# Eight heads' output matmuls in one bank: all products of the rows first, then all products of the state, one clearing matmul for each half of the partitions

## The chip, the cores and the metric

The kernel runs on one core of a Trainium2 chip. The metric is the device time of one execution in microseconds (us); the figure that counts is the median of the timed runs. All profile rows come from one profiled execution of the kernel before.

## The reference, cut to what matters

The model is two blocks of 256 tokens with 1024 channels. The second block has a recurrent layer (the function `wkv7_scan`) with 16 heads of 64 channels. Per head there is a 64 x 64 state, and for each token

```
sa = einsum('bhij,bhj->bhi', S, a_t)
S = S * w_t + sa[..., None] * b_t + v_t[..., None] * k_t
y_t = einsum('bhij,bhj->bhi', S, r_t)
```

The kernel computes this in chunks of 64 tokens. For a chunk and a head the output y is a sum of two products: one of the chunk's own rows (values v and corrections u, against a masked 128 x 64 matrix), and one of the state that the chunk before left behind (64 x 64, against the chunk's queries). The first chunk has no state, so it has the first product alone.

## The kernel before, in words

The program is traced as one long list of instructions for each engine, and a planner puts each engine's list in an order at build time: an instruction that was traced earlier goes first when it is ready by the planner's reckoning, and a later one may fill a gap. On the chip each engine takes its list in that order.

Work runs through these stages: the first block, a feed-forward layer, the recurrent layer (function `rwkv`), feed-forward, feed-forward, attention, feed-forward. The change touches the last part of `rwkv`. There the 16 heads are two halves A = 0 and A = 1 of eight heads. These generators are stepped in a written order, the string `OB`:

- `chain(A)` is the recurrence over the four chunks, in order: L1150 (state times a, on TensorE), L1152 (VectorE adds it into the tile `u`), L1157 (inverse times u), L1159 (ScalarE copies the result back into `UV`), L1165 (the new state's increment), L1173 (VectorE makes the new state).
- `outputs(A)` takes, for each chunk `ch`, a PSUM bank, runs the matmuls for eight heads (four pairs `i`, two heads `e` of a pair in the two halves of the partitions), and has ScalarE copy the bank into `Y` (L1188). L1185 is the product of the rows: 128 rows of contraction, 64 columns of output, written "128*64" in the rows. L1187 is the product of the state: 64 rows, 64 columns, "64*64"; e = 0 uses the upper left quarter of the array, e = 1 the lower right one.
- `finish(j)` turns `Y` into the layer's normalised and gated output (L1223 transposes, L1232 centring, L1236 and L1237 gate, L803 sums of squares, then VectorE and ScalarE).
- `out_part` multiplies by the output weights (L126, three products per weight block).

```
OB="cocooocccfccfccOffcOOOFFppppFFqqrr"
RB={..., "o": "AAB", "t": "AAB", "fv": "AAB", "fc": "C", "fg": "AAB", ...}
env = {"c": chain(1), "o": outputs(0), "f": chained(finish(0), finish(1)), "p": p0, "O": outputs(1),
       "F": chained(finish(2), finish(3)), "q": part(1), "r": part(2)}
```

So `o` are the four chunks of the first half's outputs, `O` those of the second half; three of the four `O` stand in a row, and behind them `F` and then `p`. `OB` is the tracing order; the planner keeps near to it. The banks of `o` and `O` go round A, A, B (two buffers of A, one of B). All these operands are 32-bit floats; a matmul of such operands shows as two records of MATMUL in the trace (and two of LDWEIGHTS).

A matmul with `start=True` clears the bank's accumulation in the partitions it writes, one without adds to what was written since the last clearing, or overwrites where nothing was.

Of the kernel before, what the change touches and what calls it, by code (L numbers as in the profile page):

```python
# [49 lines left out]
class Builder:  # L50
# [759 lines left out]
    def rwkv(self, x, ss):  # L810
        nc, tc, a = self.nc, self.tc, self.a
        self.banks = {**BANKS, **RB}
        LC = float(np.exp(-0.5))
        with tc.tile_pool(name="rwkv", bufs=1) as pool:
# [114 lines left out]
            AR = [five(ARb[c // 4])[:, c % 4] for c in range(NC)]  # L929
# [119 lines left out]
            UVp, UV = [], []  # L1049
# [9 lines left out]
            PM = [None, None]  # L1059
# [117 lines left out]
            def outputs(A):  # L1177
                hp0 = 4 * A
                for ch in range(4):
                    par, cp, S = ch % 2, ch // 2, states[A][ch]  # L1180
                    by = self.bank("o")[:, :T].rearrange("p (i t) -> p i t", i=4)
                    for i in range(4):
                        for e in range(2):
                            er, h = slice(64 * e, 64 * e + 64), 2 * (hp0 + i) + e
                            nc.tensor.matmul(by[er, i], UV[ch][:, h], PM[A][1][:, ch, 2 * i + e], start=True, stop=S is None)  # L1185
                            if S is not None:
                                nc.tensor.matmul(by[er, i], S[er, i], AR[hp0 + i][er, ch, 1], start=False, stop=True)  # L1187
                    nc.scalar.activation(Y[:, hp0:hp0 + 4, 64 * ch:64 * ch + 64], by, AF.Copy)  # L1188
                    yield

# [13 lines left out]
            def finish(j):  # L1204
# [40 lines left out]
                for e in range(2):  # L1245
# [6 lines left out]
            part = lambda i: self.out_part(x, a["rk_o"], i, yh, yl)  # L1252
            p0 = part(0)
            env = {"c": chain(1), "o": outputs(0), "f": chained(finish(0), finish(1)), "p": p0, "O": outputs(1),
                   "F": chained(finish(2), finish(3)), "q": part(1), "r": part(2)}
            for o in OB:
# [293 lines left out]
```

## Time and profile before

| what | us |
|---|---|
| median of 3 runs | 2389.93 |
| the runs | 2403.57, 2389.93, 2389.66 |
| profiled execution | 2403.91 |
| its span, first to last instruction | 2401.9 |
| TensorE busy in the span | 2286.2 |
| VectorE busy | 1558.1 |
| ScalarE busy | 1086.7 |

The profiled execution is 14.0 us above the median. Times in the rows count from the start of its span. "PE" is TensorE, "DVE" VectorE, "ACT" ScalarE, "POOL" GpSimd. PEclk is the granted clock of TensorE as a share of 2.4 GHz (0.50 is 1.2 GHz).

### The profile page before, as it was taken

The page shows a single profiled execution, that of the slowest core. Times are in us where ns is not written, and L with a number is a line of the kernel's source. Part 1 is how long each engine was busy: PE and PEld are TensorE (multiplying, and loading weights), DVE is VectorE, ACT ScalarE, POOL GpSimd, SP SyncE. Part 2 cuts the span into 40 slices and gives each one's busy share as a digit, 9 for nine tenths or more (in the row PEclk, how much of TensorE's full clock was granted, in tenths as well). Part 3 has the DMA queues.
Part 4 walks back from the last instruction along what each step waited for, and adds up shares of the span by engine and source line. Part 5 has one row for each costly group of instructions (what it writes and reads, how often), then busy time and mean ns, then how long its engine had stood idle before and what let it go on. Part 6 is the DMA issues. An engine that isn't in the chain of part 4 may idle for free.

```text
span 2401.9 us, 48629 instructions
## 1 busy us (share of the span) xinstructions
PE 2286.2 (95%) x20688; PEld 2171.1 (90%) x20688; DVE 1558.1 (65%) x2387; ACT 1086.7 (45%) x1501; POOL 319.1 (13%) x226
## 2 busy tenths in 40 slices
PE   4999898999999989999999789999999999999999
PEld 3888898999999989999999678878999999888999
DVE  7667579448854497555765777325665765787664
ACT  4344444443344433445544554423544644555543
POOL 3001379500000000000000543211000000101000
PEclk7889899999999999999999788967999999999999
DMA  7766444554455535555556222202556556433555
GB/s 252 243 197 201 150 159 158 189 180 141 143 187 187 179 115 163 187 185 167 175 185 178 83 91 64 84 1 70 181 181 187 182 185 184 155 106 107 185 185 148
DMA packets 107756, 378.33 MB, mean 158 GB/s; under 512 B 12113, under 2 KB 15697, under 8 KB 107410
## 3 DMA queue, kind: packets, MB, share of 16 engines
q1 hardware_dynamic: 104224, 370.52, 48.2%
q10 hardware_dynamic: 3314, 4.70, 0.6%
q8 instruction: 162, 2.65, 0.5%
q14 instruction: 56, 0.46, 0.1%
HBM read 374.12 MB, written 1.05 MB: 156 GB/s over the span
## 4 chain that ended last, share of the span: by engine, by line
PE 77%; DVE 6%; POOL 2%; ACT 1%; issue 1%; POOLq 0%; DVEq 0%; ACTq 0%
PE bkA L126 25%; PE bkA L572 15%; PE bkB L126 11%; PE bkC L750 10%; PE bkD L750 4%; DVE wlo L100 1%; POOL wlo L100 1%; POOL b L865 1%; PE bkC L1349 1%; DVE e L718 1%; PE bkA L1185 1%; ACT whi L99 1%; PE bkB L731 0%; PE bkE L731 0%; DVE ep L722 0%
## 5 line engine op out<-in xcount | busy, mean ns | idle before, releaser
L99 ACT ACTIVATE whi<-raw 128x1024 fp32r<-128x1024 f32 (+1 forms) x664 | 695.6, 1048 | 999.7 <-PE bkA L126 284.8
L100 DVE TENSOR_TENSOR wlo<-raw,whi 128x1024 fp32r<-128x1024 f32 (+1 forms) x606 | 733.4, 1211 | 480.1 <-ACT whi L99 449.7
L126 PE MATMUL bkA<-xh,whi 128*128 128x256 f32 x1336 | 332.0, 287 | 14.8 <-ACT whi L112 7.0
L126 PE MATMUL bkA<-xl,whi 128*128 128x256 f32 x1336 | 331.4, 288 | 12.4 <-POOL xl L316 6.3
L126 PEld LDWEIGHTS bkA<-xh,whi 128*128 128x128 f32 x1336 | 255.7, 192 | 18.2 <-ACT whi L112 7.7
L126 PEld LDWEIGHTS bkA<-xl,whi 128*128 128x128 f32 x1336 | 255.5, 193 | 16.3 <-POOL xl L316 8.7
L572 PE MATMUL bkA<-xh,whi 128*128 128x256 f32 x1024 | 259.9, 290 | 0.0
L572 PE MATMUL bkA<-xl,whi 128*128 128x256 f32 x1024 | 251.6, 281 | 0.0
L572 PEld LDWEIGHTS bkA<-xl,whi 128*128 128x128 f32 x1024 | 193.3, 189 | 0.0
L572 PEld LDWEIGHTS bkA<-xh,whi 128*128 128x128 f32 x1024 | 193.2, 189 | 0.0
L126 PE MATMUL bkA<-xh,wlo 128*128 128x256 f32 x1336 | 187.4, 282 | 2.5 <-DVE wlo L100 2.5
L100 POOL TENSOR_TENSOR wlo<-raw,whi 128x1024 fp32r<-128x1024 f32 x58 | 155.6, 2694 | 197.0 <-DVE on L149 128.7
L126 PEld LDWEIGHTS bkA<-xh,wlo 128*128 128x128 f32 x1336 | 171.0, 190 | 3.1 <-DVE wlo L100 2.9
L126 PE MATMUL bkB<-xh,whi 128*128 128x256 f32 x624 | 157.3, 289 | 1.9 <-ACT whi L99 1.1
L572 PE MATMUL bkA<-xh,wlo 128*128 128x256 f32 x1024 | 149.7, 284 | 7.5 <-POOL wlo L100 7.5
L126 PE MATMUL bkB<-xl,whi 128*128 128x256 f32 x624 | 156.2, 288 | 0.0
L572 PEld LDWEIGHTS bkA<-xh,wlo 128*128 128x128 f32 x1024 | 132.2, 188 | 8.9 <-POOL wlo L100 8.9
L190 POOL TENSOR_TENSOR sq<-sq,sq 128x256 f32<-128x256 f32 (+1 forms) x15 | 17.5, 1164 | 902.0 <-ACT sq L188 685.0
L126 PEld LDWEIGHTS bkB<-xh,whi 128*128 128x128 f32 x624 | 120.8, 194 | 2.6 <-ACT whi L99 1.4
L126 PEld LDWEIGHTS bkB<-xl,whi 128*128 128x128 f32 x624 | 120.8, 194 | 0.2 <-issue 0.2
L126 PE MATMUL bkA<-hh,whi 128*128 128x256 f32 x484 | 117.8, 282 | 0.0
L126 PE MATMUL bkA<-hl,whi 128*128 128x256 f32 x484 | 117.5, 281 | 0.0
(649 smaller groups left out, 4533.8 us busy)
## 6 DMA issues: line engine op xcount, KB each, us to landing
raw<-in_ffn_in_dram SPq DMA_DIRECT2D x176, 512.0 KB, 3.5
raw<-in_peer_u_dram SPq DMA_DIRECT2D x128, 512.0 KB, 3.3
raw<-in_peer_v_dram SPq DMA_DIRECT2D x128, 512.0 KB, 3.7
raw<-in_ffn_out_dram SPq DMA_DIRECT2D x64, 512.0 KB, 3.6
rawm<-in_w_mod_dram SPq DMA_DIRECT2D x48, 512.0 KB, 4.3
raw<-in_w_in_dram SPq DMA_DIRECT2D x36, 512.0 KB, 4.5
raw<-in_ffn_out_dram SPq DMA_DIRECT2D x32, 384.0 KB, 3.1
raw<-in_w_query_dram SPq DMA_DIRECT2D x16, 512.0 KB, 3.3
```

The source lines that it names most:

```text
L99: nc.scalar.activation(hi[:, :n], raw[:, :n], AF.Copy)
L100: (lo_eng or nc.vector).tensor_tensor(lo[:, :n], raw[:, :n], hi[:, :n], op=ALU.subtract)
L126: nc.tensor.matmul(out, w[:, i], x[k0 + i], start=first and n == 0, stop=last and n == 3 * kn - 1)
L190: (nc.vector if c % 2 else nc.gpsimd).tensor_tensor(acc[c % 2], acc[c % 2], t, op=ALU.add)
L572: last = nc.tensor.matmul(out, w[:, i], x[i], start=j == 0, stop=j == 3 * NC - 1)
L718: nc.vector.tensor_tensor(e, idx[:, ts].rearrange("p (a b) -> p a b", b=2)[:, :, None].to_broadcast(shape), iota[:, None, i0:i0 + e.shape[ ...
L750: nc.tensor.matmul(acc[db // 2][:, (db % 2) * T:(db % 2 + 1) * T], vs[:, db * 128:(db + 1) * 128], ws[:, e], start=n == 0 and p == 0 and d ...
L865: nc.gpsimd.tensor_tensor(ll[:, c], t, hh[:, c], op=ALU.subtract)
L1185: nc.tensor.matmul(by[er, i], UV[ch][:, h], PM[A][1][:, ch, 2 * i + e], start=True, stop=S is None)
L1349: nc.tensor.matmul(o, qn[pr, h, 128 * i:128 * i + 128], kn[pr, h, :w], start=True, stop=False)
```

## The change

The loop over heads in `outputs` is split in two. Before, each head had its product of the rows (clearing) and right behind it its product of the state (adding). After, the eight products of the rows are issued first; only the first of each half of the partitions (i = 0) clears, the others are written without clearing. Then the eight products of the state are issued. Number, shapes and operands of the matmuls, the bank and the copy by ScalarE are the same.

```diff
-                    for i in range(4):
-                        for e in range(2):
-                            er, h = slice(64 * e, 64 * e + 64), 2 * (hp0 + i) + e
-                            nc.tensor.matmul(by[er, i], UV[ch][:, h], PM[A][1][:, ch, 2 * i + e], start=True, stop=S is None)
-                            if S is not None:
-                                nc.tensor.matmul(by[er, i], S[er, i], AR[hp0 + i][er, ch, 1], start=False, stop=True)
+                    ie = [(i, e, slice(64 * e, 64 * e + 64)) for i in range(4) for e in range(2)]
+                    for i, e, er in ie:
+                        nc.tensor.matmul(by[er, i], UV[ch][:, 2 * (hp0 + i) + e], PM[A][1][:, ch, 2 * i + e],
+                                         start=i == 0, stop=S is None and i == 3)
+                    for i, e, er in ie if S is not None else ():
+                        nc.tensor.matmul(by[er, i], S[er, i], AR[hp0 + i][er, ch, 1], start=False, stop=i == 3)
```

## Rows read from the trace of the kernel before

**Rows 1.** The page: its busy times, and its chain that ended last.

```profile
PE 2286.2 (95%) x20688; PEld 2171.1 (90%) x20688; DVE 1558.1 (65%) x2387; ACT 1086.7 (45%) x1501; POOL 319.1 (13%) x226
...
PE 77%; DVE 6%; POOL 2%; ACT 1%; issue 1%; POOLq 0%; DVEq 0%; ACTq 0%
```

**Rows 2.** Instructions of L1185 and L1187: durations in ns, minimum/median/maximum, times.

```profile
L1185 PE MATMUL bkA<-b,b x96: 222/314/367, 1564.2 to 1634.4; 128*64 128x64 f32 x96
...
L1185 PE MATMUL bkB<-b,b x32: 222/292/367, 1572.3 to 1620.9; 128*64 128x64 f32 x32
...
L1187 PE MATMUL bkA<-b,t2c x16: 218/242/268, 1567.0 to 1571.4; 64*64 64x64 f32 x16
```

**Rows 3.** Table by stage: window, length, busy by engine, PEclk, DMA share, GB/s.

```profile
1584.08:1615.05 30.97, 30.97 (x172) 20.45 (x170) 7.80 (x15) 5.48 (x12) 7.14 (x7) 0.50 0.00 1
1615.05:1635.02 19.97, 19.97 (x102) 14.23 (x101) 5.09 (x9) 3.39 (x8) 0.00 (x0) 0.50 0.00 1
1635.02:1643.45 8.43, 8.43 (x21) 5.08 (x21) 0.87 (x2) 1.97 (x5) 3.09 (x3) 0.50 0.00 0
1643.45:1650.00 6.55, 6.55 (x44) 6.46 (x43) 3.97 (x6) 2.32 (x3) 0.00 (x0) 0.76 0.01 1
1566.70:1584.08 17.38, 17.03 (x194) 13.34 (x191) 2.78 (x8) 1.95 (x4) 0.62 (x1) 0.93 0.01 2
```

**Rows 4.** Timeline of PE, second half's last three output groups: start, length, instruction.

```profile
1615.05 0.47 PE L1185 MATMUL bkB<-b,b 128*64 128x64 f32 x2
1615.45 0.47 PE L1187 MATMUL bkB<-b,t2f 64*64 64x64 f32 x2
...
1635.02 1.22 PE L1236 MATMUL bkB<-tg,b 128*128 128x256 f32 x2
1636.17 1.22 PE L1237 MATMUL bkB<-tgb,t2b 32*128 32x256 f32 x2
```

**Rows 5.** Timeline of PE, first half's output groups.

```profile
1572.73 0.33 PE L1185 MATMUL bkB<-b,b 128*64 128x64 f32 x2
1572.99 0.33 PE L1187 MATMUL bkB<-b,t2c 64*64 64x64 f32 x2
...
1581.99 0.47 PE L1187 MATMUL bkA<-b,t2d 64*64 64x64 f32 x2
1582.39 0.47 PE L1185 MATMUL bkA<-b,b 128*64 128x64 f32 x2
```

**Rows 6.** Chain of waits in order of time: start, length on the chain, what.

```profile
1563.16 1.07 PE bkD L1157 x16
...
1571.82 0.62 PE bkC L1165 x16
...
1575.24 0.43 DVE b L1152
...
1578.43 0.60 ACT b L1159
...
1587.14 1.05 PE bkE L1165 x16
...
1599.67 1.04 PE bkA L1185 x14
...
1613.22 1.90 PE bkD L1157 x16
```

**Rows 7.** Timeline of PE where L1150 runs on two quarters of the array in turn.

```profile
1594.27 0.31 PE L1150 MATMUL bkD<-t2f,b 64*64 64x64 f32 x1
1594.33 0.31 PE L1150 MATMUL bkE<-t2f,b 64*64 64x64 f32 x1
```

**Rows 8.** Timeline of DVE behind the second half's outputs: idle before it, releaser.

```profile
1640.98 0.87 DVE L130 TENSOR_TENSOR b<-b,b 128x256 fp32r<-128x256 f32 x2 [18.98 <-ACT b L129]
```

**Rows 9.** Timeline of PE in a later call of `finish`, at 2.4 GHz.

```profile
1660.57 0.70 PE L1236 MATMUL bkA<-tg,b 128*128 128x256 f32 x2
1661.20 0.69 PE L1237 MATMUL bkA<-tgb,t2b 32*128 32x256 f32 x2
```

## The prediction

> **What bounds the kernel now.** I read the page first: TensorE is busy 95% of the span, and the chain that ended last lies on it for 77% [rows 1]. Then the table by stage, for the end of the recurrent layer: from 1566.70 to 1650.00 TensorE has work in all but 0.35 of 83.3 us, VectorE and ScalarE are mostly idle, and the DMA is at rest (a share of 0.01 at most) [rows 3]. A microsecond that TensorE sheds here should therefore be one less in the total, unless another engine becomes late.
>
> Then the two lines themselves. L1185 has 128 records, two for a matmul: 64 matmuls, eight in each of eight groups. L1187 has 16 records in each of six lists of this form: 48 matmuls, in the six groups that have a state [rows 2]. In those groups the two lines take turns, 96 matmuls in all, and the timeline shows at which pace: one starts 0.26 us after the other while the clock is at 2.4 GHz, 0.40 us after it at 1.2 GHz [rows 4, 5]. The second half's last three groups stand back to back: 19.97 us for 48 matmuls and four short transposes, 6.45 us a group [rows 3, 4].
>
> The same shapes go much faster where the tile shape doesn't change between neighbours. L1165 (128*64, two column halves in turn, as in L1185) takes 0.62 us for 16 records at 2.4 GHz and 1.05 us at 1.2: 0.08 and 0.13 us a matmul. L1185 itself, in the one group without a state, needs 1.04 us for 14 records at 1.2 GHz [rows 6]. So each change between 128*64 and 64*64 costs about 0.26 - 0.08 = 0.18 us at 2.4 GHz and 0.40 - 0.13 = 0.27 us at 1.2. A group with a state has 16 such changes now.
>
> **The change, part by part.** *Fewer changes of tile shape.* The matmuls stay; a group keeps two changes, one between its halves and one at its edge. What is not in the trace is eight state products in a row, alternating between the upper left and lower right quarters. Their upper bound is L1157: 16 records of 64*64 on a single quarter, 1.07 us at 2.4 GHz and 1.90 us at 1.2 [rows 6]. Their lower bound is the alternation of L1150 between two quarters, one record every 0.055 us at 1.2 GHz, so 0.9 us for 16 [rows 7]. I take L1165's 0.62 and 1.05 us: there too two records run on one tile and two on the other, and the halves written are the same.
>
> A group then costs 1.05 + 1.05 + 2 x 0.27 = 2.64 us at 1.2 GHz (3.49 with L1157's price) in place of 6.45, and 0.62 + 0.62 + 2 x 0.18 = 1.60 us at 2.4 GHz (2.05) in place of 16 x 0.26 = 4.16.
>
> - Second half, three groups at 1.2 GHz: 3 x (6.45 - 2.64) = 11.4 us (8.9 with the dear price).
> - First half, two groups at 2.4 GHz: 2 x (4.16 - 1.60) = 5.1 us; the third ran from 1579.08 to 1584.08, partly after the clock fell: 5.0 - 1.6 = 3.4 us. Together 8.5 us (7.2).
>
> *What is late next.* In the first half the recurrence runs beside these groups. Its third chunk can't be put out before the chain has made it: from the L1157 that begins at 1567 this is four matmul blocks (three at L1157's 1.07 us at most, one L1165 at 0.62), two ScalarE steps of 0.60 and three VectorE steps of 0.43 [rows 6], 6.3 us, so 1573.3. TensorE's own work up to that point is 1579.08 - 1566.7 - 5.1 = 7.3 us, so 1574.0. The two nearly meet; for the steps of other engines that then show I take 1 us off (0 to 3). In the second half no chain is needed in the three groups: the last L1157 ended before them. What follows, `finish`, starts with gate matmuls that need none of these outputs [rows 4], and they cover ScalarE's copy. VectorE's part of `finish(1)` is done at 1622.0 and then VectorE idles 18.98 us, until TensorE's progress releases ScalarE [rows 8]; 11.4 us less leaves 7.6 us of that. So neither becomes the bound. ScalarE's copies, the banks' turns and the DMAs aren't touched: the three groups use three different buffers, as now.
>
> *One clearing matmul per half.* It removes no instruction and adds no wait; I cost it at nothing, since a matmul's duration in the one group that clears every time (L1185 without a state) is that of L1165, which clears too, and no row separates the two flags. If not clearing had a price it would show in those 48 matmuls; nothing in the trace bounds it but the pace of L1187, which never clears.
>
> Sum: 11.4 + 8.5 - 1.0 = 18.9 us, with the dear ends 8.9 + 7.2 - 3 = 13.1. Against the profiled execution that is 2403.9 - 18.9 = 2385.0. This execution was 14.0 us above the median of the runs; I carry the difference over: 2389.9 - 18.9 = 2371.0 us.
>
> **The rivals.** *The clock stays up (W).* In the profiled execution the clock is at 2.4 GHz until about 1581.7 (a mean of 0.93 over the 17.38 us that end at 1584.08) and at 1.2 from there until some 3 us into the dense L126 (0.76 over those 6.55 us) [rows 3, 5]. What TensorE did before the fall was the alternation, with the fewest matmuls per microsecond of the stage; before the rise it had begun L126. After the change the first half's groups are dense, and the matmuls per microsecond go up, so the cause of the fall may be gone. Against it: in the following 31 us TensorE was busy without a pause at 1.2 GHz, and the clock didn't come back [rows 3], so that mix may not hold it either. The price: pairs of L1236 and L1237 follow each other at 1.15 us at 1.2 GHz and 0.63 at 2.4 [rows 4, 9], a factor of 0.55. The stage of 30.97 us would take 17.0 (14.0 less), the three groups 4.8 instead of 7.9 (3.1 less), the 8.43 us of `finish` 4.6 (3.8 less), and the beginning of L126, half of 6.55 us at the low clock, 1.5 less: 22.4 us on top. That is 2362.6 for the profiled execution. If the 14.0 us between executions come from elsewhere, the median would be 2348.6. If they come from this very stage (14.0 us is what those 31 us are worth), the quicker runs have part of it already, and the median would be 2362.6 as well. So 2349 to 2363.
>
> *The gain is swallowed (H).* The second half's gain doesn't reach the end: the planner orders differently, the steps of `finish` and of the chain on VectorE and ScalarE show in full, or the quicker runs have the second half's stage at 2.4 GHz already and lose it after. Then only the first half's 7.5 us or less remain: 2382 to 2389. Against it speaks VectorE's idle time [rows 8].
>
> *State products collide (C), slower.* The state products of a pair use two row tiles and write one bank, which the recurrence avoids by giving L1150's two quarters different banks. If such neighbours had to wait for each other, with a stall each, the second loop would be dear. It decides from (6.45 - 1.05 - 0.54) / 8 = 0.61 us per state product at 1.2 GHz, and (4.16 - 0.62 - 0.36) / 8 = 0.40 at 2.4. With twice the present pace, 0.80 and 0.52 us, a group would cost 8.0 and 5.1 us, 3 x 1.54 + 3 x 0.98 = 7.6 us more in all: 2397.5. For it there is no row: L1157 costs 0.13 and 0.24 us a matmul on a single quarter [rows 6].
>
> The Trainium skill has a rule that speaks for this rival: TensorEngine Tiling (Array Packing), under Restrictions and Gotchas, says that different row tiles can't use the same PSUM bank at the same time. Taken as mere taking of turns it would give the dear price of L1157, and the sum 15.1 us in place of 18.9 with the chain's allowance unchanged; no row here shows two row tiles writing one bank back to back.
>
> *Not as described.* The planner could put state products between the row products again, where it reckons those ready earlier. They add to the same bank, though, and both of their operands are older than the row products'; what can come between are the chain's matmuls, which have one of the two shapes. I count this in H.
>
> **How the numbers follow.** The forecast has 0.50, W 0.36, H 0.11, C 0.03. The forecast's own range is 2366 to 2377 (the dear prices at one end, a clock that falls a few microseconds later at the other). The range takes in W's lower figure and part of H: 2349 to 2383, which leaves out C, half of H and what may lie under W, together less than 0.2. About 1%, 23.9 us, is what a measurement of this kernel tells from no change; faster by more means below 2366.0. All of W but a little does that, and the low edge of the forecast: 0.40. Slower by over 1% (above 2413.8) would take a collision far above the one priced: 0.02. Within 1%: 0.58.
>
> **What the changed profile would show.** Each output group as one run of L1185 x16 and one of L1187 x16, about 1.6 us at 2.4 GHz or 2.6 at 1.2; the three groups of the second half in about 8 us (5 at 2.4 GHz) in place of 20; 0.08 to 0.13 us per state product at 2.4 GHz if L1165 is the right price, more if the two quarters take turns. The stage between the halves tells forecast from W: 31 us with a granted clock of 0.50, or about 17 us with 1.00. The prediction is wrong if the state products run above 0.24 us each, if TensorE shows new idle time of several microseconds behind the groups, or if the quicker runs had a different clock in this stage than the profiled one.

## The result, and the profile after

The changed kernel takes 2350.34 us in the median of 5 runs (2346.53 to 2357.28), the kernel before 2389.66 us (5 runs, 2388.59 to 2403.57): a ratio of 0.984, 95% interval [0.982, 0.987], a gain of 39.3 us. The forecast was a gain of 18.9 us. The time lies in the predicted range, near the lower figure of the rival W (2348.6), which I held less likely than the forecast.

The page of the changed kernel, its busy times and its chain; beside [rows 1], TensorE is busy 59.1 us less in as many instructions, and is as much the bound as before:

```profile
PE 2227.1 (95%) x20688; PEld 2130.1 (91%) x20688; DVE 1558.9 (66%) x2387; ACT 1085.5 (46%) x1501; POOL 320.4 (14%) x226
...
PE 77%; DVE 6%; POOL 2%; ACT 2%; issue 1%; POOLq 0%; DVEq 0%; ACTq 0%
```

In the changed kernel the rows' products are L1184, the state's products L1187. The list of instructions of L1184, for [rows 2]: the median record goes from 314 to 222 ns, which was its minimum before.

```profile
L1184 PE MATMUL bkA<-b,b x96: 222/222/270, 1548.8 to 1581.1; 128*64 128x64 f32 x96
```

The table by stage, in the columns of [rows 3]. The cuts are starts of instructions on TensorE: the first output product, the first centring matmul (L1232), the first of the second half's three groups in a row, the gate matmul behind them (L1236), the first weight product of `out_part` (L126), and the first one of the next feed-forward layer.

```profile
1548.85:1561.29 12.44, 12.03 (x268) 10.85 (x267) 3.62 (x9) 3.55 (x8) 1.24 (x2) 1.00 0.01 3
1561.29:1577.57 16.28, 16.28 (x154) 11.07 (x151) 7.53 (x15) 4.75 (x11) 7.25 (x7) 1.00 0.00 1
1577.57:1581.85 4.28, 4.13 (x102) 3.59 (x101) 2.92 (x6) 3.23 (x8) 0.00 (x0) 1.00 0.02 4
1581.85:1586.39 4.54, 4.54 (x24) 2.96 (x21) 3.30 (x7) 1.97 (x5) 2.22 (x3) 1.00 0.00 0
1586.39:1615.11 28.72, 28.70 (x218) 26.25 (x217) 26.66 (x39) 14.03 (x22) 4.34 (x4) 1.00 0.36 107
```

The granted clock is 1.00 in all five: 2.4 GHz from the first output group to the next feed-forward. In the profiled execution of before, three of these parts are in [rows 3] at 0.50. Between the same cuts:

| part | before, us (PEclk) | after, us (PEclk) | less |
|---|---|---|---|
| first half, to the first centring | 21.75 (0.90) | 12.44 (1.00) | 9.3 |
| between the halves | 29.13 (0.50) | 16.28 (1.00) | 12.9 |
| three groups of the second half | 19.97 (0.50) | 4.28 (1.00) | 15.7 |
| `finish` behind them | 8.43 (0.50) | 4.54 (1.00) | 3.9 |
| `out_part`, to the next feed-forward | 30.15 (0.95) | 28.72 (1.00) | 1.4 |
| sum | 109.43 | 66.26 | 43.2 |

The timeline of TensorE over the three groups, for [rows 4, 5, 9]; start, length, instruction:

```profile
1577.57 0.69 PE L1184 MATMUL bkB<-b,b 128*64 128x64 f32 x16
1578.18 0.68 PE L1187 MATMUL bkB<-b,t2f 64*64 64x64 f32 x16
1578.79 0.69 PE L1184 MATMUL bkA<-b,b 128*64 128x64 f32 x16
1579.41 0.68 PE L1187 MATMUL bkA<-b,t2f 64*64 64x64 f32 x16
1580.24 0.46 PE L1223 MATMUL bkB<-c_ident,b 64*128 64x64 f32 x4
1580.62 0.69 PE L1184 MATMUL bkA<-b,b 128*64 128x64 f32 x16
1581.24 0.68 PE L1187 MATMUL bkA<-b,t2g 64*64 64x64 f32 x16
1581.85 0.70 PE L1236 MATMUL bkB<-tg,b 128*128 128x256 f32 x2
1582.48 0.69 PE L1237 MATMUL bkB<-tgb,t2b 32*128 32x256 f32 x2
```

A group has become one run of 16 records and another of 16, each start 0.61 us after the one before it: 1.22 us a group, where 16 steps of 0.26 us made 4.16 at the same clock. And VectorE, whose idle time [rows 8] was the cover for the second half, in the timeline of the changed kernel at the same step:

```profile
1585.60 0.92 DVE L130 TENSOR_TENSOR b<-b,b 128x256 fp32r<-128x256 f32 x2 [1.07 <-ACT b L129]
```

Of 18.98 us of idle time 1.07 are left; the cover was nearly used up, but not over. ScalarE did come onto the chain of waits: from 1577.67 to 1580.20 us the chain lies on it, up to its copy out of bank B (L1188), and the transposes L1223, which write bank B next, start behind that copy. TensorE idles 0.15 us there (4.13 of 4.28 us busy in the table).

```profile
1579.92 0.28 ACT b L1188
...
1580.24 0.46 PE bkB L1223 x4
```

The two profiled executions differ by 57.4 us, more than the medians. 43.2 are the table's. 15.3 lie ahead of the first output group (1564.16 against 1548.85), where both kernels have the same instructions in the same order, and -1.1 behind the table. So the 14.0 us by which that execution of before exceeded the median remained to be explained.

### The profile page after: what moved, and what is told of

The parts are those of the page before. It is cut to its first block, busy times and chain, and to the rows that moved or that the text cites. A ratio compares the mean times of both kernels' runs of the same rounds, so it can differ in the third digit from the quotient of the medians.

```text
span 2344.5 us, 48629 instructions
## 1 busy us (share of the span) xinstructions
PE 2227.1 (95%) x20688; PEld 2130.1 (91%) x20688; DVE 1558.9 (66%) x2387; ACT 1085.5 (46%) x1501; POOL 320.4 (14%) x226
## 4 chain that ended last, share of the span: by engine, by line
PE 77%; DVE 6%; POOL 2%; ACT 2%; issue 1%; POOLq 0%; DVEq 0%; ACTq 0%
PE bkA L126 26%; PE bkA L572 15%; PE bkB L126 11%; PE bkC L750 11%; PE bkD L750 4%; DVE wlo L100 1%; POOL wlo L100 1%; POOL b L865 1%; PE bkC L1349 1%; DVE e L718 1%; ACT whi L99 1%; PE bkB L731 1%; DVE ep L722 1%; PE bkE L731 1%; DVE A L737 0%
## 5 line engine op out<-in xcount | busy, mean ns | idle before, releaser
L126 PE MATMUL bkA<-xh,whi 128*128 128x256 f32 x1336 | 331.0, 286 | 15.2 <-ACT whi L112 7.4
L126 PE MATMUL bkA<-xl,whi 128*128 128x256 f32 x1336 | 330.8, 288 | 12.4 <-POOL xl L316 6.3
L126 PEld LDWEIGHTS bkA<-xh,whi 128*128 128x128 f32 x1336 | 254.9, 192 | 18.6 <-ACT whi L112 8.1
L126 PEld LDWEIGHTS bkA<-xl,whi 128*128 128x128 f32 x1336 | 254.9, 192 | 16.3 <-POOL xl L316 8.7
L126 PE MATMUL bkA<-xh,wlo 128*128 128x256 f32 x1336 | 188.5, 284 | 2.4 <-DVE wlo L100 2.4
L126 PEld LDWEIGHTS bkA<-xh,wlo 128*128 128x128 f32 x1336 | 172.3, 191 | 3.1 <-DVE wlo L100 2.8
L126 PE MATMUL bkB<-xh,whi 128*128 128x256 f32 x624 | 155.7, 287 | 1.5 <-ACT whi L99 0.7
L126 PE MATMUL bkB<-xl,whi 128*128 128x256 f32 x624 | 153.9, 285 | 0.0
L126 PEld LDWEIGHTS bkB<-xh,whi 128*128 128x128 f32 x624 | 119.6, 192 | 2.2 <-ACT xh L208 1.2
L126 PEld LDWEIGHTS bkB<-xl,whi 128*128 128x128 f32 x624 | 119.1, 192 | 0.2 <-issue 0.2
L126 PE MATMUL bkA<-hh,whi 128*128 128x256 f32 x484 | 117.9, 282 | 0.0
L126 PE MATMUL bkA<-hl,whi 128*128 128x256 f32 x484 | 117.5, 281 | 0.0
```

The source lines that it names most:

```text
L126: nc.tensor.matmul(out, w[:, i], x[k0 + i], start=first and n == 0, stop=last and n == 3 * kn - 1)
```

## The experiments

**The kernel before, profiled again, and each half alone.** Theory T: matmuls of two tile shapes in turns bring the clock down, and regrouping keeps it up. Theory P: the low clock of the first profile was a chance of that execution, and the regrouping gains by its own matmuls alone. The first kernel is the one before, unchanged.

> The kernel before, unchanged, for a second profile of it. Theory T (the turn-taking groups make the clock fall, and what follows keeps the level it enters with): the stage between the halves is again at a granted clock of 0.50 in most of its 31 us, whatever the 14 us between executions are; they then lie ahead of this stage. Theory P (the clock's fall is a chance of the single execution, and the change itself is worth only the 18.9 us of the sum): an execution near 2389 us should show the stage between the halves at 1.00, about 17 us long, and the 14 us there.

2394.41 us (10 runs), ratio to the kernel before 1.000 [0.997, 1.003]. The table by stage, cut where the clock changes:

```profile
1552.00:1559.00 7.00, 6.98 (x114) 5.83 (x111) 1.62 (x4) 1.57 (x3) 1.24 (x2) 1.00 0.01 2
1559.50:1583.20 23.70, 23.68 (x177) 18.44 (x176) 2.51 (x6) 3.00 (x8) 2.57 (x3) 0.50 0.00 1
1583.40:1600.20 16.80, 16.80 (x150) 11.44 (x148) 8.34 (x17) 5.87 (x13) 4.47 (x5) 1.00 0.01 1
1600.40:1627.50 27.10, 27.10 (x113) 19.14 (x113) 5.94 (x11) 4.38 (x10) 3.08 (x3) 0.50 0.00 1
```

T's 31 us at 0.50 between the halves did not come again; there P is right. But P's difference between executions isn't all in this place either. The clock falls earlier, in the first half's first group with a state; it comes back between the halves, where no group takes turns; it falls again in the first of the three groups (the step from one matmul to the next goes from 0.26 to 0.40 us at 1600.5). From the first output group to the next feed-forward it is 102.4 us in place of 109.4. Of the 17.8 us between these two executions (2403.91 and 2386.12) only 7.0 lie in this part.

The next two kernels regroup one half only; the other keeps its turns.

```diff
+                    rows = lambda i, e, er, **k: nc.tensor.matmul(
+                        by[er, i], UV[ch][:, 2 * (hp0 + i) + e], PM[A][1][:, ch, 2 * i + e], **k)
+                    state = lambda i, e, er, **k: nc.tensor.matmul(
+                        by[er, i], S[er, i], AR[hp0 + i][er, ch, 1], **k)
+                    if A == 0:
+                        for i, e, er in ie:
+                            rows(i, e, er, start=i == 0, stop=S is None and i == 3)
+                        for i, e, er in ie if S is not None else ():
+                            state(i, e, er, start=False, stop=i == 3)
+                    else:
+                        for i, e, er in ie:
+                            rows(i, e, er, start=True, stop=S is None)
+                            if S is not None:
+                                state(i, e, er, start=False, stop=True)
```

> Regrouped in the first half's outputs alone; the second half takes turns as before. T: the first half's end and the stage between the halves stay at 2.4 GHz (8.8 us and 13.5 us less than in the kernel before), and the clock falls somewhere in the second half's three groups, since these take turns: 20 to 26 us less than before in all. P: 7 to 9 us less than before, the stage between the halves 31 us at 0.50.

2371.16 us (10 runs), 0.992 [0.990, 0.995]. Its table by stage: the first half and the part between the halves are those of the changed kernel to 0.01 us, and the clock stays at 2.4 GHz until the second half's turns have begun. The interval of the ratio is a gain of 12.7 to 23.9 us, which leaves out P's 7 to 9.

```profile
1551.30:1563.74 12.44, 12.02 (x268) 10.86 (x266) 3.62 (x9) 3.56 (x8) 1.24 (x2) 1.00 0.01 3
1563.74:1580.01 16.27, 16.27 (x153) 11.06 (x150) 7.53 (x15) 4.75 (x11) 7.26 (x7) 1.00 0.00 1
...
1580.18:1585.40 5.22, 5.22 (x42) 3.81 (x41) 3.72 (x8) 2.56 (x6) 0.00 (x0) 0.99 0.01 3
1585.60:1597.17 11.57, 11.57 (x59) 8.28 (x60) 1.34 (x3) 0.88 (x3) 0.00 (x0) 0.50 0.00 0
```

The second half alone is the same edit with `A == 1`:

> Regrouped in the second half's outputs alone. T: the clock falls at the first half's third group as before and stays at 1.2 GHz until the dense L126; the three groups of the second half take 3 x 2.64 = 8 us in place of 20: 11 to 12 us less than before. P: the same 11 to 12 us less. A gain of 20 us or more would speak against T, since then the first half's turn-taking would not be what lowers the clock.

2363.0 us (4 runs), 0.990 [0.984, 0.996], a gain of some 24 us, twice what either theory gave it. By what was said ahead of the run, 20 us or more speak against T. The table shows against which half of T: not against the turns as what lowers the clock, but against the clock staying at the level to which it fell. Here the clock falls in the third of the first half's groups, as in the first profile of before, but is back 6.8 us later, and the second half runs at 2.4 GHz:

```profile
1557.56:1575.40 17.84, 17.47 (x239) 14.10 (x238) 3.62 (x9) 2.93 (x6) 1.24 (x2) 1.00 0.01 2
1575.60:1582.20 6.60, 6.60 (x52) 5.05 (x52) 0.39 (x1) 1.61 (x4) 1.85 (x2) 0.51 0.00 0
1582.40:1596.84 14.44, 14.44 (x130) 9.70 (x129) 6.86 (x14) 3.87 (x8) 5.20 (x6) 1.00 0.00 1
1596.84:1601.18 4.34, 4.19 (x104) 3.65 (x103) 2.97 (x6) 3.23 (x8) 0.00 (x0) 1.00 0.02 4
```

**One group in turns.** The changed kernel, but with the condition `(A, ch) != (0, 3)` in the edit above, so that the last chunk of the first half takes turns again.

> The changed kernel, but the first half's third group with a state (16 of the 96 matmuls) takes turns as before. Its own price is 14 changes of tile shape at 0.18 us, 2.5 us. T, strictly (this group is what lowers the clock): the clock falls in it and stays down to L126, 20 to 25 us slower than the changed kernel. T, loosely (all three groups together are too sparse, one alone is not): the clock stays, 2 to 3 us slower than the changed kernel. P: 2 to 3 us slower too, whichever the clock.

2366.93 us (6 runs), 0.989 [0.985, 0.992]. Cut at that group, which begins at 1568.64:

```profile
1559.01:1568.60 9.59, 9.22 (x208) 8.25 (x203) 3.52 (x9) 2.72 (x6) 1.24 (x2) 1.00 0.02 3
1568.60:1572.50 3.90, 3.86 (x30) 2.92 (x30) 0.10 (x1) 0.00 (x0) 0.00 (x0) 0.96 0.00 0
1572.70:1579.40 6.70, 6.70 (x48) 4.91 (x48) 0.42 (x1) 2.20 (x5) 3.50 (x4) 0.53 0.00 0
1579.60:1593.50 13.90, 13.90 (x141) 9.65 (x140) 7.43 (x14) 3.56 (x8) 3.56 (x3) 1.00 0.00 1
```

The clock falls inside this one group and comes back at about 1579.0. First output group to feed-forward: 72.0 us, 5.7 more than in the changed kernel. About 2.9 of them are the turns (4.16 - 1.22 us); the rest, 2.8, I put down to the low clock. So turns do bring the clock down (T), but a single group doesn't keep it down through the next part, against what I had expected of T; neither the 20 to 25 us nor the 2 to 3 us came. By the medians this kernel is further from the changed one, 16.6 us (2366.93 against 2350.34, not measured side by side). Of the 13.9 us between the two profiled executions (2360.43 and 2346.53) 9.8 lie ahead of the part (its first output product is at 1558.64 in place of 1548.85), where both kernels have the same instructions. So the 5.7 us are the reading of one profile, and the medians are too coarse to confirm it.

**What a change of shape costs, and what else is lost.** In the changed kernel 16 records take 0.61 us. Two theories for the price: with D it is all in the changes of tile shape, and dense matmuls cost the same in any order; with O the two halves of the array also work at the same time when their matmuls are neighbours. The first kernel changes shape after each pair (two halves of one shape, then two of the other), and clears at each rows' product.

```diff
+                    for i in range(4):
+                        ie = [(e, slice(64 * e, 64 * e + 64)) for e in range(2)]
+                        for e, er in ie:
+                            nc.tensor.matmul(by[er, i], UV[ch][:, 2 * (hp0 + i) + e], PM[A][1][:, ch, 2 * i + e],
+                                             start=True, stop=S is None)
+                        for e, er in ie if S is not None else ():
+                            nc.tensor.matmul(by[er, i], S[er, i], AR[hp0 + i][er, ch, 1], start=False, stop=True)
```

> Per pair of heads: both row products (each clearing), then both state products; 8 changes of tile shape in a group where the kernel before has 16 and the changed one 2. Theory D (only the change costs, 0.18 us each, as the prediction has it): a group with a state takes 16 x 0.08 + 8 x 0.18 = 2.7 us at 2.4 GHz. Theory O (a stretch of one shape costs about 0.15 us to begin, and after that two matmuls on the two halves of the array run at once, 0.058 us a record pair, so that taking turns costs the overlap as well): each pair costs what a single matmul costs in the kernel before, 0.256 us, and a group 2.05 us. In both the clock should stay at 2.4 GHz if it is the sparseness that lowers it; 5 to 9 us slower than the changed kernel, 30 us quicker than before.

2361.73 us (4 runs), 0.990 [0.985, 0.995]; first output group to feed-forward 71.6 us, the clock at 1.00 throughout. The timeline of TensorE (rows' products L1185, state's products L1188):

```profile
1592.32 0.34 PE L1185 MATMUL bkB<-b,b 128*64 128x64 f32 x4
1592.59 0.33 PE L1188 MATMUL bkB<-b,t2f 64*64 64x64 f32 x4
1592.85 0.34 PE L1185 MATMUL bkB<-b,b 128*64 128x64 f32 x4
...
1594.43 0.34 PE L1185 MATMUL bkA<-b,b 128*64 128x64 f32 x4
```

Eight steps, one group, in 2.11 us, close to O's 2.05 and not D's 2.7. That is 0.264 us for four records, where before two records took 0.256: ten steps in 2.56 us at 2.4 GHz, here from the timeline of the second profile of before ([rows 5] show one step).

```profile
1597.67 0.33 PE L1185 MATMUL bkB<-b,b 128*64 128x64 f32 x2
...
1600.23 0.33 PE L1185 MATMUL bkB<-b,b 128*64 128x64 f32 x2
```

The second matmul of a pair comes almost free. Against the changed kernel the part is 5.4 us longer, as six groups at 2.11 in place of 1.22 us make it; the medians, on one chip, differ by 13.1 us (2348.59 for the changed kernel), more than the 5 to 9 expected. Of the 15.1 us between those two profiled executions 9.9 lie ahead of the part. The second kernel keeps the changed kernel's two changes of shape but runs the four matmuls of one half before the four of the other:

```diff
-                    ie = [(i, e, slice(64 * e, 64 * e + 64)) for i in range(4) for e in range(2)]
+                    ie = [(i, e, slice(64 * e, 64 * e + 64)) for e in range(2) for i in range(4)]
```

> The changed kernel with the loop over the halves outside: four row products of the upper half, four of the lower, then the state products likewise; two changes of tile shape as in the changed kernel, but neighbours now share a tile. D: no difference, 1.22 us a group. O: no overlap of neighbours, 16 records at 0.058 us a product list, 2 x (0.15 + 0.93) = 2.2 us a group; 6 x 1.0 = 6 us slower than the changed kernel.

2355.41 us (4 runs), 0.988 [0.984, 0.992]; 69.0 us, the clock at 1.00.

```profile
1585.89 0.97 PE L1184 MATMUL bkB<-b,b 128*64 128x64 f32 x16
1586.79 0.96 PE L1187 MATMUL bkB<-b,t2f 64*64 64x64 f32 x16
1587.68 0.97 PE L1184 MATMUL bkA<-b,b 128*64 128x64 f32 x16
```

0.89 to 0.90 us for the 16 records that take 0.61 with the halves in turn. D, which said 1.22 us a group, falls; O's 2.2 was too high, the group takes 1.79. The three numbers can be solved. Let a matmul that overlaps with no other cost m, a pair of matmuls on both halves p, a change of shape c. Before: m + c = 0.256. Pairs: p + c = 0.264. Changed: 4p + c = 0.61. So p = 0.115, c = 0.15 and m = 0.11 us: a pair takes as long as one matmul. Half by half without any overlap would then be 8m + c = 1.0 us; it measured 0.9. So these prices are good to about 0.1 us in 1; something may still overlap where one half hands over to the other, but no run here shows it.

A place in the changed kernel gives c by itself. Where L1165 and L1184, of one shape, stand together, 32 records take 1.08 us up to the next line's start, with one change of shape; two runs of different shapes above took 1.22, with two:

```profile
1554.21 0.69 PE L1165 MATMUL bkC<-b,b 128*64 128x64 f32 x16
1554.73 0.64 PE L1184 MATMUL bkB<-b,b 128*64 128x64 f32 x16
1555.29 0.33 PE L1187 MATMUL bkB<-b,t2c 64*64 64x64 f32 x2
```

The difference, 0.14 us, is one change.

**Clearing.** The changed order with every product clearing; this kernel leaves out the product of the rows from its result, since the product of the state clears it.

```diff
-                                         start=i == 0, stop=S is None and i == 3)
+                                         start=True, stop=True)
...
-                        nc.tensor.matmul(by[er, i], S[er, i], AR[hp0 + i][er, ch, 1], start=False, stop=i == 3)
+                        nc.tensor.matmul(by[er, i], S[er, i], AR[hp0 + i][er, ch, 1], start=True, stop=True)
```

> The changed kernel's order, but each of the 16 products of a group clears (so the group's output is the product of the state alone; the product of the rows is overwritten). If clearing is free, a group is again 1.22 to 1.23 us, the part from the first output group to the next feed-forward 66.3 us, the clock 1.00 in it, and the time that of the changed kernel, 2346 to 2352 us. If the one clearing matmul for each half is a part of the gain, a group costs more: 0.02 us for each of the 14 additional clearings would be 1.5 us a group, 68 us for the part. If writing without clearing is the dearer, a group is shorter than 1.22.

2353.04 us (4 runs), 0.985 [0.982, 0.989]. The whole part is 66.26 us, the changed kernel's to the last digit, the clock is at 1.00, and the groups keep their pace:

```profile
1576.91 0.69 PE L1184 MATMUL bkB<-b,b 128*64 128x64 f32 x16
1577.53 0.68 PE L1187 MATMUL bkB<-b,t2f 64*64 64x64 f32 x16
1578.14 0.69 PE L1184 MATMUL bkA<-b,b 128*64 128x64 f32 x16
```

Clearing costs nothing and not clearing saves nothing, as I had costed it; the one clearing matmul for each half is part of how the new order accumulates, not of the gain. Nor is it the clearing at each of the rows' products that lowers the clock in the kernels with turns.

**Is the changed kernel's clock a matter of luck, and is the one before's?** The changed kernel again, and the one before a third time.

> The changed kernel, unchanged, for a second profile and more runs. If it is the dense groups that keep the clock, the stage is again at 2.4 GHz from the first output group to L126, some 66 us long; 2346 to 2358 us. If the first profile was a lucky execution, the clock falls somewhere in the stage and the stage is 70 us or longer.

2348.59 us (4 runs), 0.985 [0.981, 0.990]. The part is 66.25 us with the clock at 1.00, as in all the other profiles with the changed groups.

> The kernel before, for a third profile. If the clock in this part is a matter of chance in each execution, the part from the first output group to the next feed-forward lies again between 102 and 110 us (102.5 and 109.5 in the two profiles so far) with the clock falling in a group that takes turns, and the remaining difference in time lies ahead of it. If one of the two earlier profiles was an exception, it repeats the other within 1 us.

One run, 2391.86 us. The table by stage, in the cuts of the first table:

```profile
1558.44:1586.04 27.60, 27.56 (x268) 22.04 (x266) 3.71 (x9) 3.78 (x8) 1.25 (x2) 0.63 0.01 1
1586.04:1603.87 17.83, 17.83 (x153) 12.12 (x151) 7.53 (x15) 4.62 (x11) 7.25 (x7) 0.90 0.00 1
1603.87:1622.31 18.44, 18.44 (x103) 13.20 (x101) 5.42 (x10) 3.40 (x8) 0.00 (x0) 0.57 0.00 1
1622.31:1630.74 8.43, 8.43 (x21) 5.08 (x21) 0.88 (x2) 1.97 (x5) 3.09 (x3) 0.50 0.00 0
1630.74:1660.85 30.11, 30.08 (x218) 27.57 (x217) 26.71 (x38) 14.03 (x22) 3.41 (x3) 0.95 0.33 102
```

Sum 102.41 us: the second profile again (102.44), though this execution took 5.7 us more. So of the three profiles of before, the one that I predicted from is the one that differs. Against these two the change takes 36.2 us off this part: 15.2 in the first half, 14.2 in the three groups, 3.9 in `finish`, 1.4 in `out_part`, and only 1.6 between the halves.

**The same step elsewhere.** The scores of both attention layers also alternate between shapes (64*128 with 128*128), in the second attention also between 32-bit and 16-bit operands. Their products were grouped by kind, with one clearing matmul for each bank, on top of the changed kernel; the second attention's lines:

```diff
-                    for c in range(2):
-                        h = 2 * m + c
-                        for i, o in ((0, S0[:, c]), (1, S1[:, c])):
-                            w = 128 * (i + 1)
-                            nc.tensor.matmul(o, qn[pr, h, 128 * i:128 * i + 128], kn[pr, h, :w], start=True, stop=False)
-                            nc.tensor.matmul(o, ids[:, h], abb[:, 128 * i:128 * i + w], start=False, stop=True)
+                    sc = [(2 * m + c, c, i, o, 128 * (i + 1)) for i, Si in ((0, S0), (1, S1))
+                          for c, o in ((0, Si[:, 0]), (1, Si[:, 1]))]
+                    for h, c, i, o, w in sc:
+                        nc.tensor.matmul(o, qn[pr, h, 128 * i:128 * i + 128], kn[pr, h, :w], start=c == 0, stop=False)
+                    for h, c, i, o, w in sc:
+                        nc.tensor.matmul(o, ids[:, h], abb[:, 128 * i:128 * i + w], start=False, stop=c == 1)
```

> The changed kernel, with the scores of both attentions regrouped too: there products of 64 rows and a mask or position product of 128 rows take turns, 8 changes in a block of two heads; regrouped there are 2. Sixteen blocks, 6 changes fewer each, at 0.15 us: up to 14 us less than the changed kernel where TensorE is the bound there, nothing where the softmax on VectorE is; between 0 and 14 us, and some more if the clock, which falls in the first attention, stays up.

2342.72 us (4 runs), 0.984 [0.980, 0.988], beside the changed kernel's 2348.59 on the same chip. Both once more:

> The changed kernel, unchanged, for more executions beside e9 on one chip: a median of 2346 to 2351 us, the recurrent layer's end 66.3 us long with the clock at 2.4 GHz throughout.

> The kernel with the scores of both attentions regrouped as well, unchanged, for more executions: 5 us less than e8 if the second attention's 5.3 us that its first profile showed is all, up to 8 us less if the first attention gains too; the same median as e8 if the gain was the clock of single executions.

The changed kernel 2350.09 us (6 runs), 0.983 [0.980, 0.985]; with the attentions 2347.66 (6 runs), 0.981 [0.978, 0.983]. The second attention, from its first score matmul to its last, in the changed kernel's third profile and then in the second profile with the scores grouped:

```profile
2035.78:2118.98 83.20, 81.41 (x515) 66.86 (x514) 65.00 (x141) 46.60 (x109) 0.00 (x0) 0.96 0.29 96
```

```profile
2043.40:2122.79 79.39, 77.31 (x541) 68.22 (x540) 65.99 (x140) 46.66 (x106) 0.00 (x0) 0.98 0.33 107
```

3.8 us less there shows in the profiles; in the medians it was 5.9 us in one comparison and 2.4 in the other, with intervals that overlap. The version is the quickest measured, but its lead over the changed kernel isn't settled by these runs.

## Why the prediction was wrong

**Right:** that a microsecond which TensorE sheds in this part is one less in the total. The changed kernel has 0.41 us of idle TensorE in the first half (12.44 against 12.03 us), the kernel before had 0.37 (21.75 against 21.38). So no engine became late, but for the 0.15 us behind ScalarE's copy in the three groups, where a bank's turn that I had taken as untouched comes in: the 1.0 us that I took off for the chain's steps was not paid. Rival H fell: one of its conditions came, since the second and third profile of before have the stage between the halves at 2.4 GHz and lose it after, but the second half's gain reached the end all the same. The planner kept the groups as written, but for matmuls of the chain between them in the first half.

**The step that failed is the clock.** I took the clock as the profiled execution had it (low from 1581.7 until L126), priced the second half's dense groups at 1.2 GHz, and so put what the change does to the clock at nothing. In its place the runs showed 2.4 GHz through the whole part once every group is regrouped. The argument for it, that "in the following 31 us TensorE was busy without a pause at 1.2 GHz, and the clock didn't come back", rested on one execution. In two more profiles of before the clock does come back in that very stage (0.90 between the halves), which is one of the signs of being wrong that I had named; in the kernel with one group in turns it comes back too, after 6.8 us. What W said, that the turns are the cause of the fall, is what that one group showed: clock up before it, down inside it. No profile in which every group is regrouped has a low clock in this part: eight of eight, those of pairs and of half by half included. All six profiles with groups in turns have a fall in such a group, though not in each of them.

What that step cost depends on the profile of before that one sets against the change. Against the two others it is little between the halves (1.6 us), but 3.9 in `finish` and 1.4 in `out_part`, which the forecast had at nothing, and a part of the 15.2 in the first half (forecast 7.5) and of the 14.2 in the three groups (11.4).

W's terms against the first profile: 12.9 us measured between the halves where W had 14.0, 3.9 in `finish` (3.8), 1.4 at the beginning of L126 (1.5). The first half gained 9.3 (forecast 8.5 less 1.0), the three groups 15.7 (11.4, and 3.1 more with W). W was right in the mechanism; that the median lies within 2 us of its lower figure is in part luck, since W's whole gain, 41.3 us, was worked out on the first profile, and from the two others the change takes 36.2.

**Mis-sized: a group at 2.4 GHz.** The forecast had 0.62 + 0.62 + 2 x 0.18 = 1.60 us; it is 1.22. L1165's 0.62 us on the chain of waits counts from the end of the work ahead of it, L1150 of another shape: one change was in it already, and adding two for the group counted them twice. In three groups that is 1.1 us, about what the three groups gained over the forecast with W (15.7 against 14.5). The price at 1.2 GHz, 2.64 us, was never seen, as no dense group ran at that clock.

**The 14.0 us between executions** do not come from this stage alone: between the first two profiles of before 7.0 us of 17.8 do, and 11.9 lie ahead of the first output group (1564.16 against 1552.24; -1.1 behind). That place varies among kernels with the same instructions ahead of it, from 1548.20 (every product clears) to 1560.82 (pairs). The clock differs there too: from 1350 to 1400 us it was 0.70 in the first profile of before and 0.93 in the changed kernel's. How much of the difference that makes was not taken apart. My forecast carried the whole difference over; that was harmless for a gain that both kinds of execution have, and not for one that depends on their clock. With the 102.4 us of two of the three profiles the table gives 36.2 us, with the first profile's 109.4 it gives 43.2; the medians' 39.3, [31, 44] by the interval of the ratio, lies between them.

**Rival C** is out: state products on two quarters of the array that write one bank run at the pace of the rows' products, 0.61 us for 16 records. The Trainium skill, TensorEngine Tiling (Array Packing), Restrictions and Gotchas, would not let different row tiles use one PSUM bank at once; the two quarters here write different partitions of the bank, and a pair of them takes about as long as one (steps of 0.264 against 0.256 us). The measurement decides.

**Open:** why the clock stayed low between the halves in the first profile of before, and why it fell two groups earlier in the two others. The instructions are the same. The mean clock ahead of the part differs (0.95 in the first and the third profile, 0.97 in the second), but not as the falls do, in which the second and the third agree.

## What to carry to other kernels

Where small matmuls of two tile shapes take turns, group them by shape, and within a group alternate the two halves of the array: the turns cost the change (0.15 us each here) and the overlap of the halves. Before a forecast is priced at the granted clock of one profiled execution, profile the kernel before a second time: here the part in question differed by 7 us between executions, with its clock. And before a change of shape is added to a dense run's price, see what stands ahead of the run: one change may be in it already.

## What the hardware showed that I had not expected

- TensorE busy without a pause does not keep its clock: 23.68 of 23.70 us busy at a granted clock of 0.50 in the second profile of before, and 6.98 of 7.00 us ahead of that fall. What came ahead of each fall in this part was a row of single matmuls in turns, 0.26 us apart; what came ahead of each rise was work without turns, though in the first profile of before the same work between the halves brought no rise. Matmuls per microsecond, by which the prediction put it, don't separate the two: gate matmuls are fewer, one every 0.63 us in the changed kernel, and run with the clock up. The Trainium skill, TensorE: Matmul & The Clock Gate, section "HAM oscillation — how this bites in real kernels", tells of waits of TensorE as the cause. Ahead of that fall the profile shows none, but it models the ends of matmuls.
- A pair of matmuls on the two halves of the array, neighbours in the list, costs 0.008 us more than one of them (0.264 against 0.256 us with a change of shape each).
- One group of sixteen matmuls in turns cost 5.7 us in the part, in one profile: about 2.9 for itself, and the remaining 2.8 with the low clock, most of it in the work behind it.
- Clearing the bank or not makes no difference to a matmul's pace: 66.26 us for the part either way.
